# Inverse root by whole columns, sums and residual on GpSimd, held weights joining a step later, at the phase borders of a two-block layer kernel

## The chip, the cores and the metric

One core of one Trainium2 chip runs the whole kernel. The metric is the device time of one execution in microseconds; the time before is the median of three runs. A difference of about 0.3% (some 4.8 us) is what the measurement of this kernel can tell from none.

## The reference

Two transformer-like blocks are applied in turn to x (1 batch, 512 tokens, 1024 features), all in float32. What matters at the borders between the phases is only this:

```
# block 1 (g_t, g_c, sh_c, sc_c come from the conditioning vector c)
x = x + g_t * rms_norm(token_mixer(h, ...), tm_post_g)
h = rms_norm(x, cm_pre_g) * (1 + sc_c) + sh_c
x = x + g_c * rms_norm(conv_ffn(h, ...), cm_post_g)
# block 2
h = x
h = h + hybrid_mixer(rmsnorm(h, norm_mix_g), ...)
h = h + conv_ffn_2(rmsnorm(h, norm_ffn_g), ...)
return rmsnorm(h, norm_final_g)
```

Every normalisation needs 1/sqrt(mean of squares over the 1024 features + 1e-6) for each token. The token mixer has four branches (mLSTM, gated linear attention, a convolution branch and a short convolution); two of them, and the layer norm of the third, use the same root for their own norms.

## The kernel before, in words

Activations lie with features on the 128 partitions and tokens along the free dimension: 8 feature tiles of 128x512. A product with a weight is done in three TensorE products of rounded parts (high x high, high x low, low x high), so each weight tile of 128x1024 is loaded by a DMA that SyncE issues (`wraw`), copied by ScalarE into its high part (line 119) and subtracted by VectorE into its low part (line 120). `wload` does this through rings of three buffers; `hold` and `Group` do it into buffers kept for a while.

The instructions are put into each engine's queue by the Tile scheduler, at build time, from the order of the program and a model of what each instruction takes; each queue then runs in that fixed order on the chip. An instruction at the head of a queue that waits holds everything behind it.

There are three borders that the change concerns, each between the last product of one phase and the first of the next:

- border 1: end of the token mixer (`wo`), start of the first FFN (`up1`), near 484 to 537 us
- border 2: end of the first FFN (`dn1`), start of the second block's projections (`w2`), near 845 to 908 us
- border 3: end of the second mixer (`wo2`), start of the second FFN (`up2`), near 1214 to 1263 us

At each, the last few output tiles (4, 3 and 4) are done for tokens 0 to 255 and then for 256 to 511 (`HALVES`), so that the norm of the first half can run while TensorE works on the second.

`Post.add` (line 285 on) takes one output tile from PSUM. ScalarE writes y scaled by the gain (line 296) and two squares (lines 298, 301), VectorE adds the squares to two sums (lines 299, 302) and the product y*x to a third (lines 304, 305). `Post.rows` sums the three over the partitions on TensorE (`colsum`, line 240, a 128x1 product for each 128 tokens), takes two roots one after the other (`rsqrt`) and spreads them over the partitions by transposes on TensorE (`rowcast`, line 247). `advance` then adds the normed y to x (lines 917, 918, VectorE) and `normed` makes the next phase's input in two parts (lines 923, 927 and 928, or 923, 119 and 120).

`Group` (line 174 on) is the first product of the next phase: six weight tiles against each input tile k as soon as it is there. Three tiles come from `wload`; the other three are `slots`, split into memory that is free only once the phase before is over: at border 1 two tiles of the pool `sp4` and one tile of the FFN's activation buffer, at border 2 three tiles of `sth`/`stl`, at border 3 three tiles of the activation buffer. `step(k, half)` takes one slot from the list, issues its DMA and its two split instructions, appends it to the tiles in use, and then issues the products of all tiles in use, a newly joined tile catching up on the steps it has missed. In the second half the steps 4 to 6 are left to the last one, so that the six tiles finish one after another.

`rsqrt` (line 213 on) makes s = scale*src + eps, a first guess from the bits of s by two integer instructions, and then three Newton steps. For one or two columns it uses, for each column by itself, two VectorE instructions per step with a per-partition scalar (lines 227, 228); for more columns three instructions per step over all columns (lines 231 to 233). It is called with two columns at the borders (ten times), with four, eight or sixteen in the start and in the mixer of block 1 (five times), with one at the end (four times).

GpSimd has only memsets, a cast and causal masks to do. The temporaries of `Post.add` come from a ring: three buffers at border 1; at border 2 five, of which the three sums hold three.

## Time and profile before

| | us |
|---|---|
| median of 3 runs (1598.73, 1601.64, 1603.09) | 1601.64 |
| the profiled execution, its own time | 1603.05 |
| its span, first to last instruction | 1601.3 |
| TensorE busy in the span | 1568.9 (98%) |
| VectorE busy | 1083.4 (68%) |
| ScalarE busy | 677.5 (42%) |
| GpSimd busy | 15.9 (1%) |
| mean granted TensorE clock | 0.993 |

Line numbers are those of the kernel before. A row of a timeline gives the start in us from the span's start, the length, the engine, the line, the operation, the output tile and the input tiles by their names in the program, the shape, the count, and in square brackets how long the engine was idle before it and what ended that idle time. "PE" is TensorE, "DVE" VectorE, "ACT" ScalarE, "POOL" GpSimd. Two instructions that follow each other in a queue overlap at their edges, so the distance from start to start is what one of them takes from the engine, and it is a little shorter than the length shown.

### The profile page before, as it was taken

Reading aid. Unit: us, or ns where it says so; the run is one execution under the profiler, and the core shown is the slowest. Engines: PE = TensorE matmul, PEld = TensorE weight load, DVE = VectorE, ACT = ScalarE, POOL = GpSimd, SP = SyncE. Lnnn points to the kernel's source line nnn. Section 1 sums busy time; section 2 is a strip of 40 time slices with the busy share of each in tenths; the row PEclk is TensorE's granted clock in tenths of the full one; section 3 lists DMA queues with packets and bytes.
Section 4 is the critical chain, followed back from the end, with each engine's and each line's share of the span. In section 5 each row is a group of like instructions: output and inputs, shape, how many; then the busy total and the mean of one; then the engine's idle time right before and its main releaser. Section 6 shows DMA issues by size and latency. Waiting matters only on the chain.

```text
span 1601.3 us, 20852 instructions
## 1 busy us (share of the span) xinstructions
PE 1568.9 (98%) x8015; PEld 1316.4 (82%) x8015; DVE 1083.4 (68%) x2066; ACT 677.5 (42%) x1040; POOL 15.9 (1%) x43
## 2 busy tenths in 40 slices
PE   6999999999999999999999999999999999999997
PEld 4777888888889888888899978888889988888886
DVE  7786897657778865665358899977556565665234
ACT  4456432223463544443244463448343444444122
POOL 0000100000000000000000000000000000000000
PEclk9999999999999999999999999999999999999999
DMA  8411335554550223233345222220241232232331
GB/s 305 170 53 67 106 115 187 184 170 153 177 169 17 79 97 100 92 100 91 96 134 187 75 66 89 83 93 27 79 152 59 80 100 98 92 104 81 98 113 53
DMA packets 50963, 175.91 MB, mean 110 GB/s; under 512 B 5920, under 2 KB 6192, under 8 KB 50864
## 3 DMA queue, kind: packets, MB, share of 16 engines
q1 hardware_dynamic: 50864, 174.58, 33.3%
q8 instruction: 63, 1.03, 0.3%
q14 instruction: 36, 0.29, 0.1%
HBM read 172.46 MB, written 2.10 MB: 109 GB/s over the span
## 4 chain that ended last, share of the span: by engine, by line
PE 90%; DVE 5%; ACT 3%; DMA 1%; issue 1%; SPq 0%; ACTq 0%; DVEq 0%
PE acc L131 23%; PE acc L132 23%; PE acc L133 23%; PE acc L197 3%; PE acc L1340 3%; PE tp L1340 2%; PE pc L1250 1%; PE pa L197 1%; PE pc L197 1%; PE pb L197 1%; PE pb L1340 1%; PE pa L1340 1%; PE pc L1340 1%; DVE lo L120 1%; PE acc L157 1%
## 5 line engine op out<-in xcount | busy, mean ns | idle before, releaser
L120 DVE TENSOR_TENSOR lo<-raw,hi 128x1024 fp32r<-128x1024 f32 (+1 forms) x245 | 296.4, 1211 | 312.0 <-ACT hi L119 307.9
L131 PE MATMUL acc<-hh,hi 128*128 128x512 f32 x1208 | 474.3, 393 | 0.0
L133 PE MATMUL acc<-hh,lo 128*128 128x512 f32 x1208 | 473.1, 392 | 0.0
L132 PE MATMUL acc<-hl,hi 128*128 128x512 f32 x1208 | 473.1, 392 | 0.0
L119 ACT ACTIVATE hi<-raw 128x1024 fp32r<-128x1024 f32 (+1 forms) x245 | 257.1, 1050 | 471.1 <-PE acc L132 352.6
L131 PEld LDWEIGHTS acc<-hh,hi 128*128 128x128 f32 x1208 | 227.7, 189 | 48.9 <-issue 2.0
L132 PEld LDWEIGHTS acc<-hl,hi 128*128 128x128 f32 x1208 | 227.5, 188 | 48.6 <-issue 1.8
L133 PEld LDWEIGHTS acc<-hh,lo 128*128 128x128 f32 x1208 | 227.6, 188 | 47.5 <-issue 0.7
L131 PE MATMUL acc<-act_h,hi 128*128 128x256 f32 (+1 forms) x242 | 80.4, 332 | 0.0
L132 PE MATMUL acc<-act_l,hi 128*128 128x256 f32 (+1 forms) x242 | 80.2, 331 | 0.0
L133 PE MATMUL acc<-act_h,lo 128*128 128x256 f32 (+1 forms) x242 | 80.2, 331 | 0.0
L119 ACT ACTIVATE act_h<-ffe 128x512 fp32r<-128x512 f32 x44 | 27.7, 630 | 102.5 <-DVE ffe L968 102.5
L265 DVE SCALAR_TENSOR_TENSOR raw<-raw,cb 128x1024 f32<-128x1024 f32 x32 | 39.1, 1223 | 40.0 <-DMA raw<-in_ada_dram 40.0
L964 DVE SCALAR_TENSOR_TENSOR ffe<-acc,vec,ffe 128x510 f32<-128x510 f32 x82 | 61.2, 748 | 2.6
L967 ACT ACTIVATE ffe<-ffe 128x512 f32<-128x512 f32 x44 | 27.8, 631 | 79.5 <-DVE ffe L964 79.5
L962 DVE SCALAR_TENSOR_TENSOR ffe<-acc,vec,ffe 128x511 f32<-128x511 f32 x82 | 60.7, 742 | 0.0
L131 PEld LDWEIGHTS acc<-act_h,hi 128*128 128x128 f32 x242 | 46.0, 190 | 4.4
L133 PEld LDWEIGHTS acc<-act_h,lo 128*128 128x128 f32 x242 | 46.0, 190 | 4.3
L132 PEld LDWEIGHTS acc<-act_l,hi 128*128 128x128 f32 x242 | 46.0, 190 | 4.3
L120 DVE TENSOR_TENSOR act_l<-ffe,act_h 128x512 fp32r<-128x512 f32 x44 | 30.3, 690 | 26.5 <-ACT act_h L119 26.5
L808 DVE SCALAR_TENSOR_TENSOR cv<-u,vec,cv 128x512 f32<-128x512 f32 x60 | 43.8, 746 | 0.1
L197 PE MATMUL acc<-hl,hi 128*128 128x256 f32 x144 | 40.2, 285 | 0.0
(632 smaller groups left out, 2778.4 us busy)
## 6 DMA issues: line engine op xcount, KB each, us to landing
raw<-in_up_dram SPq DMA_DIRECT2D x88, 512.0 KB, 3.3
raw<-in_wg_dram SPq DMA_DIRECT2D x48, 512.0 KB, 3.3
raw<-in_dn_dram SPq DMA_DIRECT2D x44, 512.0 KB, 3.5
raw<-in_w_dram SPq DMA_DIRECT2D x43, 512.0 KB, 3.4
raw<-in_ada_dram SPq DMA_DIRECT2D x32, 512.0 KB, 3.4
sraw<-in_ada_dram SPq DMA_DIRECT2D x16, 512.0 KB, 5.3
raw<-in_wo_dram SPq DMA_DIRECT2D x16, 512.0 KB, 3.3
raw<-in_dn_dram SPq DMA_DIRECT2D x11, 384.0 KB, 3.2
```

The source lines that it names most:

```text
L119: A.activation(hi, src, AF.Copy)
L120: V.tensor_sub(lo, src, hi.bitcast(F32))
L131: T.matmul(out, wh_, ah, start=start, stop=False)
L132: T.matmul(out, wh_, al, start=False, stop=False)
L133: T.matmul(out, wl_, ah, start=False, stop=stop)
L197: T.matmul(a, w_, x_, start=(k == 0 and n == 0 and half == 0), stop=(k == KT - 1 and n == 2 and half == 1), skip_group_check=True)
L265: V.scalar_tensor_tensor(raw, raw, 1.0, cb, op0=ALU.mult, op1=ALU.mult, accum_out=mod[:, i:i + 1])
L808: V.scalar_tensor_tensor(cv[:, j], u0[:, j, k:k + 512], htap[:, 2 * k + j:2 * k + j + 1], cv[:, j], op0=ALU.mult, op1=ALU.add)
L962: V.scalar_tensor_tensor(t[:, 1:512], acc[:, 0:511], vcol(taps, 44 + i), t[:, 1:512], op0=ALU.mult, op1=ALU.add)
L964: V.scalar_tensor_tensor(t[:, 2:512], acc[:, 0:510], vcol(taps, i), t[:, 2:512], op0=ALU.mult, op1=ALU.add)
L967: A.activation(e[0], e[0], AF.Silu)
L1340: T.matmul(o, act[a][:, k, t], w[:, n0:n1], start=(k == 0 and i == 0), stop=(k == KF - 1 and i == 2), skip_group_check=True)
```

## The change

It has four parts.

1. `rsqrt` drops the path by single columns for two columns; the last two of the three Newton steps become one step of third order with constants built from RK. The number of instructions goes from 16 to 10 for two columns, from 10 to 9 for one (which keeps the scalar form), and from 12 to 10 for four and more.
2. In `Post.add`, for tiles of half the tokens only, the two adds of squares go from VectorE to GpSimd.
3. In `advance`, the add to x goes from VectorE to GpSimd (all 32 calls are on half the tokens).
4. In `Group.step`, a slot's DMA and split stay where they were in the program, but the tile is appended after the products of the step, so its first products are issued in the next step, where it catches up.

```diff
+RK = 1.5 ** (1.0 / 7.0)
...
         def step(self, k, half, act, nlast=4):
+            coming = None
             if self.todo:
-                w, src = self.todo.pop(0)
-                split(w[0], w[1], wraw(src))
-                self.w.append(w)
-            if half == 1 and KT - nlast <= k < KT - 1:
-                return
-            for m in range(len(self.w)):
-                for q in range(self.done[m][half], k + 1):
-                    self.mm(m, q, half, act)
-                self.done[m][half] = k + 1
+                coming, src = self.todo.pop(0)
+                split(coming[0], coming[1], wraw(src))
+            if not (half == 1 and KT - nlast <= k < KT - 1):
+                for m in range(len(self.w)):
+                    for q in range(self.done[m][half], k + 1):
+                        self.mm(m, q, half, act)
+                    self.done[m][half] = k + 1
+
+            if coming:
+                self.w.append(coming)
...
-        if n <= 2:
-
-            m = sm.tile([128, 2], F32, tag="rs_m", name="rs_m")[:, :n]
-            V.tensor_scalar(m, src, -0.5 * scale, -0.5 * EPS, op0=ALU.mult, op1=ALU.add)
-            for _ in range(3):
-                for c in range(n):
-                    yc, uc = y[:, c:c + 1], u[:, c:c + 1]
-                    V.scalar_tensor_tensor(uc, yc, m[:, c:c + 1], yc, op0=ALU.mult, op1=ALU.mult)
-                    V.scalar_tensor_tensor(yc, uc, 1.5, yc, op0=ALU.add, op1=ALU.mult)
-            return y
-        for _ in range(3):
+
+        if n == 1:
+            V.tensor_scalar(s, s, -0.5 * RK, None, op0=ALU.mult)
+            V.scalar_tensor_tensor(u, y, s, y, op0=ALU.mult, op1=ALU.mult)
+            V.scalar_tensor_tensor(y, u, 1.5 * RK, y, op0=ALU.add, op1=ALU.mult)
+            V.scalar_tensor_tensor(u, y, s, y, op0=ALU.mult, op1=ALU.mult)
+        else:
             V.tensor_tensor(u, y, y, op=ALU.mult)
-            V.scalar_tensor_tensor(u, u, -0.5, s, op0=ALU.mult, op1=ALU.mult)
-            V.scalar_tensor_tensor(y, u, 1.5, y, op0=ALU.add, op1=ALU.mult)
+            V.scalar_tensor_tensor(u, u, -0.5 * RK, s, op0=ALU.mult, op1=ALU.mult)
+            V.scalar_tensor_tensor(y, u, 1.5 * RK, y, op0=ALU.add, op1=ALU.mult)
+            V.tensor_tensor(u, y, y, op=ALU.mult)
+            V.scalar_tensor_tensor(u, u, -0.5 * RK, s, op0=ALU.mult, op1=ALU.mult)
+        V.scalar_tensor_tensor(u, u, RK ** 3 / 0.6, u, op0=ALU.add, op1=ALU.mult)
+        V.scalar_tensor_tensor(y, u, 1.25 * RK ** 6, y, op0=ALU.add, op1=ALU.mult)
         return y
...
-                V.tensor_tensor(s[0], s[0], t, op=ALU.add)
+                E = V if n == 512 else G
+                E.tensor_tensor(s[0], s[0], t, op=ALU.add)
...
-                V.tensor_tensor(s[1], s[1], t, op=ALU.add)
+                E.tensor_tensor(s[1], s[1], t, op=ALU.add)
...
         t = btmp()
         V.tensor_tensor(t, y[:, j, t0:t1], r1, op=ALU.mult)
-        V.tensor_tensor(x[:, j, t0:t1], x[:, j, t0:t1], t, op=ALU.add)
+        G.tensor_tensor(x[:, j, t0:t1], x[:, j, t0:t1], t, op=ALU.add)
```

## Rows read from the trace of the kernel before

**Rows 1.** The head of the profile's page: the span and the busy time of the engines.

```profile
span 1601.3 us, 20852 instructions
PE 1568.9 (98%) x8015; PEld 1316.4 (82%) x8015; DVE 1083.4 (68%) x2066; ACT 677.5 (42%) x1040; POOL 15.9 (1%) x43
```

**Rows 2.** The list of waits of TensorE over the whole span: the waiting line and what ended the wait, then us in total, times, longest us.

```profile
PE pc L197 <- ACT act_h L119: 1.2, 1, 1.2
...
PE pa L197 <- ACT sth L119: 0.7, 1, 0.7
...
PE pb L197 <- ACT sth L119: 0.4, 1, 0.4
```

**Rows 3.** Busy time of each engine in two stretches, one in border 1 and one in border 2: the stretch, its length, busy us and count for PE, PEld, DVE, ACT and POOL, the granted TensorE clock (1.00 is 2.4 GHz), the DMA share and GB/s.

```profile
497.00:508.00 11.00, 9.46 (x74) 8.68 (x72) 9.74 (x42) 3.92 (x8) 0.00 (x0) 1.00 0.13 40
...
868.00:882.00 14.00, 12.76 (x88) 11.95 (x88) 12.79 (x45) 5.98 (x10) 0.57 (x3) 0.88 0.66 203
```

**Rows 4.** Timeline of TensorE in border 1.

```profile
500.62 0.50 PE L240 MATMUL tp<-cst,th 128*128 128x1 f32 x4
502.32 0.38 PE L197 MATMUL pc<-hh,act_h 128*128 128x256 f32 x1 [1.20 <-ACT act_h L119]
```

**Rows 5.** Timeline of ScalarE in border 1: the split of the third slot and the instruction behind it.

```profile
501.21 1.06 ACT L119 ACTIVATE act_h<-raw 128x1024 fp32r<-128x1024 f32 x1 [2.64 <-PE tp L240]
502.17 0.49 ACT L927 ACTIVATE hh<-cb,mod 128x256 fp32r<-128x256 f32 x1
```

**Rows 6.** Timeline of VectorE in border 1.

```profile
495.27 0.42 DVE L304 TENSOR_TENSOR tmp<-y,x 128x256 f32<-128x256 f32 x1
...
496.28 0.42 DVE L305 TENSOR_TENSOR th<-th,tmp 128x256 f32<-128x256 f32 x1
496.61 0.47 DVE L923 SCALAR_TENSOR_TENSOR cb<-x,gcols,tp 128x256 f32<-128x256 f32 x1
...
499.53 0.47 DVE L923 SCALAR_TENSOR_TENSOR cb<-x,gcols,tp 128x256 f32<-128x256 f32 x1
```

**Rows 7.** Timeline of TensorE in border 2.

```profile
873.73 0.28 PE L197 MATMUL acc<-hh,lo 128*128 128x256 f32 x1
874.74 0.38 PE L197 MATMUL pa<-hh,sth 128*128 128x256 f32 x1 [0.74 <-ACT sth L119]
...
876.59 0.28 PE L197 MATMUL pa<-hl,sth 128*128 128x256 f32 x1
876.71 0.37 PE L197 MATMUL pa<-hh,stl 128*128 128x256 f32 x1
...
877.10 0.42 PE L197 MATMUL pa<-hl,sth 128*128 128x256 f32 x1
877.31 0.41 PE L197 MATMUL pa<-hh,stl 128*128 128x256 f32 x1
```

**Rows 8.** Timelines of VectorE and of ScalarE in border 2: the first two rows are VectorE's, the last two ScalarE's.

```profile
873.58 0.16 DVE L217 TENSOR_SCALAR rs_s<-tp 128x2 f32<-128x2 f32 x1 [1.19 <-PE tp L240]
...
873.85 0.47 DVE L923 SCALAR_TENSOR_TENSOR cb<-x,vec,tp 128x256 f32<-128x256 f32 x1
...
873.63 2.96 ACT L119 ACTIVATE sth<-raw 128x1024 fp32r<-128x1024 f32 x3 [3.30 <-PE tp L240]
876.49 0.40 ACT L119 ACTIVATE hh<-cb 128x256 fp32r<-128x256 f32 x1
```

**Rows 9.** Timelines of VectorE in three roots: of four columns in the convolution branch (371 us), of two columns in border 3 (1216 to 1218 us, first and last instruction, with one other instruction of 0.41 us between them), of one column at the end of the kernel (1595.7 us on), and ScalarE's first use of that one.

```profile
371.31 0.16 DVE L231 TENSOR_TENSOR rs_u<-rs_y 128x4 f32<-128x4 f32 x1
...
371.90 0.16 DVE L231 TENSOR_TENSOR rs_u<-rs_y 128x4 f32<-128x4 f32 x1
...
1215.91 0.16 DVE L217 TENSOR_SCALAR rs_s<-tp 128x2 f32<-128x2 f32 x1 [0.76 <-PE tp L240]
...
1217.75 0.41 DVE L1283 TENSOR_TENSOR x<-x,acc 128x256 f32<-128x256 f32 x1
1218.08 0.15 DVE L228 SCALAR_TENSOR_TENSOR rs_y<-rs_u,rs_y 128x1 f32<-128x1 f32 x1
...
1595.72 0.16 DVE L228 SCALAR_TENSOR_TENSOR rs_y<-rs_u,rs_y 128x1 f32<-128x1 f32 x1
1595.91 0.22 DVE L227 SCALAR_TENSOR_TENSOR rs_u<-rs_y,rs_m 128x1 f32<-128x1 f32 x1
...
1596.81 0.72 ACT L1369 ACTIVATE xt<-xt,rs_y 128x512 f32<-128x512 f32 x1 [2.14 <-DVE rs_y L228]
```

**Rows 10.** Timeline around the last root of the gated linear attention: VectorE's use of the root and the TensorE instruction that waited for it.

```profile
130.42 0.68 DVE L637 TENSOR_TENSOR go<-tp,rs_y 128x512 f32<-128x512 f32 x1
...
131.25 0.19 PE L674 MATMUL tp<-cst,rows 4*128 4x4 f32 x1 [0.81 <-DVE go L637]
```

**Rows 11.** Single lines of the program: the add to x, and one of the adds of squares (border 2's phase); engine, operation, tiles, count, then shortest, median and longest ns, first and last start, and shapes.

```profile
L918 DVE TENSOR_TENSOR x<-x,cb x32: 415/424/426, 494.9 to 898.1; 128x256 f32<-128x256 f32 x32
...
L302 DVE TENSOR_TENSOR ffe<-ffe x10: 414/417/684, 775.6 to 870.6; 128x256 f32<-128x256 f32 x6, 128x512 f32<-128x512 f32 x4
```

**Rows 12.** Timeline of GpSimd and VectorE in two places: the same masking instruction of GpSimd, once beside an instruction of VectorE that reads one of its two operands from PSUM (L732), once beside a weight split of VectorE.

```profile
161.24 0.29 POOL L721 TENSOR_SCALAR_AFFINE_SELECT x2a<-x2a 128x128 f32<-128x128 f32 x1 [0.74 <-ACT x2a L718]
...
960.84 1.22 DVE L120 TENSOR_TENSOR lo<-raw,hi 128x1024 fp32r<-128x1024 f32 x1
960.99 1.22 POOL L1116 TENSOR_SCALAR_AFFINE_SELECT mb<-mb 128x128 f32<-128x128 f32 x1 [7.14 <-DVE mb L1114]
```

## The prediction

> **What bounds the kernel now.** I read the head of the page first: TensorE is busy 1568.9 of 1601.3 us [rows 1]. So the change can only give back what TensorE waits for, and everything else is hidden. The list of TensorE's waits comes next: at the borders it names three waits for the held weights, 1.2 us at border 1 and 0.7 and 0.4 us at border 2 [rows 2]. Border 3 has no such row: there TensorE is fed. The windows of the two borders say the same from the other side: TensorE is idle 1.54 of 11 us at border 1 and 1.24 of 14 us at border 2, and in the second the granted clock is 0.88 [rows 3]. As the clock has two levels, 1.2 and 2.4 GHz, 0.88 means 3.4 of the 14 us at the lower.
>
> Then the timelines, to see who is late. At border 1 TensorE has done its column sums at about 501.1 us and starts again at 502.32 with the third slot's weights [rows 4]. ScalarE had begun that split at 501.21, because the memory came free only with the column sums, and the next tile's high part stood behind it in ScalarE's queue until 502.17 [rows 5], although its input left VectorE at 500.0 [rows 6]. So not only the weights are late: the next input tile waits behind them. At border 2 it is the same with three splits: ScalarE makes them in one piece of 2.96 us from 873.63 on, and the high part of the next input tile follows at 876.49 [rows 8]; TensorE stops at 873.85 (873.73 + 0.12) and gets its weights at 874.74 [rows 7]. VectorE is late too: it made the input of that tile at 873.85, after 1.19 us in which its queue stood at the root's first instruction, waiting for the column sums [rows 8].
>
> **Part 1, the root.** For two columns, 16 instructions become 10. That isn't six times their length. The old root ran from 1215.91 to 1218.23, less the 0.33 us of one foreign instruction in it: 1.99 us [rows 9], since the two columns' chains overlap. The new one is a chain of ten dependent instructions over whole columns. Three of these take 0.59 us (371.31 to 371.90), so 0.197 each and 1.97 us for ten [rows 9]. The root's own latency at the borders stays as it is: 0.0, with 0.2 us to either side. What it frees is VectorE's queue where other work is mixed in, and I count that under part 2. One column: one step less on the last chain. From the second half of one step to the first of the next is 0.19 us (1595.72 to 1595.91), and ScalarE's first use ends a wait of 2.14 us for the root, with nothing on TensorE [rows 9]: -0.2 us, fully on the path that sets the end. Eight columns: two instructions less, 0.39 us, ahead of the instruction at 130.42 that TensorE waits 0.81 us for [rows 10]: -0.4, between 0 (another queue entry is next) and -0.8. The other roots of four and sixteen columns stand beside TensorE's work or beside loads: 0.
>
> **Part 2, the sums on GpSimd.** 14 half tiles have two adds each: 28 leave VectorE (the row of one of the two lines shows 6 half tiles at border 2; border 1 has 8). For a half tile VectorE now needs 1.43 us from the start of its first add to the end of its last (495.27 to 496.70) [rows 6], and at border 1 such a block stood right ahead of the next phase's input at 496.61. With two of four instructions gone VectorE ends 0.68 us sooner. GpSimd's adds of two tensors have no row. The nearest are its mask over half the columns, 0.29 us by itself and 1.22 us beside a weight split of VectorE, both starting within 0.15 us [rows 12]. I take 0.6, twice the lower for twice the columns; ends 0.29 and 1.22. At 0.6 the second add ends 1.2 us after the first square is there, about where VectorE's last ended; at 1.22 it ends 1.2 us later than now. The column sums are next in TensorE's queue after that, and behind them stand the next phase's products, so a late sum is paid by TensorE. There are four such places (two halves, two borders): at 1.22 that is +5.0 us, at 0.29 -1; I take +0.2 each, +0.8 in all, because the scheduler places the sums by its model and nothing says that it fits GpSimd.
>
> The Trainium skill, GPSIMD Engine Reference, section 3.1, has 4497 ns for an add of 2048 float32 columns on GpSimd against 2293 ns on VectorE, and tells to keep such work on VectorE. An estimate from it, an eighth of that plus a fixed part, is 0.6 to 0.7 us for these adds, near the value that I take; by it the sum would come out less than half a microsecond higher. No run here shows it yet.
>
> **Part 3, the add to x.** 32 instructions of 0.42 us [rows 11] leave VectorE and one of GpSimd takes their place in the chain of each input tile. The chain gets longer by 0.2 (at 0.6) or 0.8 us (at 1.22), but VectorE's work per tile falls from four instructions to three, 1.58 to about 1.2 us. TensorE needs 18 products of 0.12 us, 2.2 us, per tile with six weights and 1.1 with three (spacing 876.59 to 876.71 [rows 7]). By the time of the column sums of the second half, VectorE has 2 us (two blocks of adds, two x adds) less to do at border 1 and as much at border 2, so one or two further input tiles, with their high parts, pass ScalarE before the splits. Each gives TensorE 9 to 15 products, 1.1 to 1.8 us. That covers the 1.20 us at border 1 (-1.2) and the 0.74 and 0.45 us at border 2 (-1.2). The cover is these tiles alone: if they don't pass, both waits stay.
>
> At border 2 the clock is the larger item. TensorE was idle 0.74 and 0.45 us, and then the spacing of its products went from 0.12 to 0.21 us (877.10 to 877.31) [rows 7]. In 3.4 us these are 16 products with 0.09 us too much: 1.5 us. With the idle gone, I take this back whole: -1.5, with 0 at the other end.
>
> **Part 4, the slots a step later.** DMA, ScalarE copy and VectorE subtraction of a slot keep their place in the program; no queue but TensorE's is passed. The products move behind those of the step, which by itself moves the wait rather than removes it: at border 1 the input tile behind the split came free at 502.66, later than the weights [rows 5]. So the step is worth what part 3 puts in front of it: 0 by itself, -0.3 to +0.3.
>
> **The sum,** against the profiled execution (1603.05, span 1601.3): -0.4 (eight columns) -0.2 (end) -1.2 (border 1) -1.2 -1.5 (border 2) +0.8 (sums) = -3.7. The profiled execution lies 1.4 above the median, so 1601.64 - 3.7 = **1597.9 us**, -0.23%. A measurement of this kernel tells a change of about 0.3%, 4.8 us, from none.
>
> **The rivals.**
>
> *The waits stay (it doesn't do what it says).* ScalarE's order is fixed when the program is built. If the splits again stand ahead of the next high part, TensorE waits as now, for the input in place of the weights. For it: rows 5 and 8, where just this happened to an input that was ready (border 1) or nearly (border 2). Against it: 2 us less on VectorE ahead of it. It leaves the root's 0.6 us and half a wait: **1601.0**. Chance 0.24.
>
> *Everything closes.* GpSimd's add is at 0.29: the four sums come sooner (-1 in place of +0.8), the linear attention's root gives its 0.8, and small waits of 0.2 go: -3.7 - 1.8 - 0.4 - 0.8 = -6.7: **1594.9**. For it: GpSimd is empty at the borders (0.57 us in 14) [rows 3]. Chance 0.18.
>
> *GpSimd is the new bound, and it is slower.* The mechanism is one: GpSimd and VectorE hold each other up where VectorE reads two operands from SBUF, as the mask beside the split shows, 1.22 in place of 0.29 us [rows 12]. Then an input tile costs 1.22 + 0.40 us one after the other (the low part reads two operands too), 1.62 against the 1.1 that three weight tiles give TensorE: 0.5 us for each of the first four tiles at two borders, 4.3 us, and +5.0 at the sums, -0.6 of the roots, no wait regained: **1610.3**. It decides from about 0.7 us for the add (1.1 - 0.40) on, and wins by more than 4.8 us from about 0.9. Against it: most of VectorE's work around the add to x (lines 917 and 923) reads one operand from PSUM, and the mask beside such work took 0.29. Chance 0.08.
>
> The Trainium skill, SBUF — State Buffer, section "SBUF: two separate sides", has the rule for this: the port pair that both engines share is a lock held for a whole instruction, against VectorE instructions with two SBUF inputs. By that rule this rival is right in kind wherever splits and low parts are mixed with GpSimd's adds; the trace agrees in the one place it shows (1.22 beside 0.29).
>
> **How the numbers follow.** The forecast has 0.50 and its own range of 1596.0 to 1600.0. Below 1596.8 (faster by 0.3%) lie the second rival's 0.18 and 0.15 of the forecast's: 0.33. Above 1606.4 lies the third, 0.08. The rest, 0.59, can't be told from no change. The range from 1593.5 to 1602.5 takes in the forecast and the first two rivals with their spread and leaves out the third and the tails, together less than 2 in 10.
>
> **What would show it.** Right: the rows of waits for act_h and sth are gone, ScalarE's splits at 501 and 873 have more high parts ahead of them, the granted clock stays 1.00 through border 2, GpSimd's adds take near 0.6 us, and the last root is 0.2 us shorter. Wrong: a wait of the column sums for a GpSimd line, a wait of TensorE for a high part that stands behind a split, GpSimd adds of 1 us and more, or a second fall of the clock at border 1. Each of these says which term failed.

## The result, and the profile after

The changed kernel takes 1618.93 us in the median, against 1602.37 us for the kernel before on the same chip: a ratio of 1.0101, 95% interval 1.0088 to 1.0115. It is slower by 16 us, and 21 us above the forecast. The median is of 1616.09, 1618.50, 1619.36 and a slow run of 2608.15 us at a mean granted clock of 0.557, which all ratios and intervals leave out, like two more further down (1730.62 us of e3_sums, and 4013.68 us of e10_ring, its profiled one, so that it has no windows in the table). The profiled execution's own time is 1616.09 us. In this section, lines are those of the changed kernel; against the listing of the kernel before they lie 1 to 4 further down (split L121, the products of `Group` L198, adds of squares L303 and L306, y*x L308 and L309, `advance` L921 and L922, next input L927, high part L931 or L120, low part L932 or L121, column sums L243, transposes L250). In the other kernels below they differ by a few lines again.

The busy times, which answer to [rows 1] (the span is 1614.4 us):

```profile
PE 1575.2 (98%) x8015; PEld 1322.4 (82%) x8015; DVE 1079.4 (67%) x1932; ACT 677.2 (42%) x1040; POOL 65.5 (4%) x103
```

134 instructions and some 25 us of adds left VectorE, and its busy time fell by only 4.0 us (from 1083.4): what stayed got longer. GpSimd took on 50 us. The list of waits of TensorE, which answers to [rows 2]:

```profile
PE acc L198 <- DVE lo L121: 3.7, 2, 2.4
...
PE tp L250 <- DVE rs_y L236: 2.2, 1, 2.2
...
PE acc L198 <- ACT tmp L301: 1.1, 1, 1.1
PE tp L243 <- POOL th L303: 0.8, 2, 0.5
...
PE tp L243 <- POOL ffe L303: 0.6, 1, 0.6
```

The three waits for held weights (2.3 us) are gone, as they were meant to. In their place stand 8.4 us at the borders: for low parts of weights (VectorE), for a root (VectorE), for a square of ScalarE and for GpSimd's sums. Busy time by engine and granted clock around the two borders, in the columns of [rows 3], but in wider stretches, so that they hold nearly the whole border of every kernel (here the last product of the `Group` at border 1 ends at 542.85 us):

```profile
480.00:540.00 60.00, 55.29 (x426) 53.57 (x425) 47.18 (x117) 19.90 (x42) 23.45 (x30) 0.94 0.07 22
845.00:925.00 80.00, 74.95 (x563) 71.94 (x562) 59.67 (x134) 30.33 (x52) 21.39 (x31) 0.94 0.40 126
```

TensorE is idle 4.71 us at border 1 and 5.05 at border 2 (kernel before, same stretches: 1.67 and 2.12), and the granted clock is 0.94 in both (1.00 and 0.98), that is at the lower of its two levels for about 7 of the 60 and 10 of the 80 us. From the first to the last product of the `Group` it takes 42.68 us at border 1 and 46.08 at border 2, against 38.88 and 39.94. Border 3, where nothing of this is on the path, takes 35.81 against 35.98.

Who got slower is in the groups of instructions (line, engine, operation, tiles, form, count; busy us and mean ns; idle us before them and what ended it):

```profile
L927 DVE SCALAR_TENSOR_TENSOR cb<-x,vec,tp 128x256 f32<-128x256 f32 x32 | 14.5, 474 | 5.7 <-POOL x L922 5.2 <-PE tp L250 0.5
L921 DVE TENSOR_TENSOR cb<-y,tp 128x256 f32<-128x256 f32 x32 | 13.1, 410 | 1.6 <-PE tp L250 1.6
L932 DVE SCALAR_TENSOR_TENSOR hl<-cb,mod,hh 128x256 fp32r<-128x256 f32 x16 | 12.4, 775 | 3.0 <-ACT hh L931 2.8
...
L308 DVE TENSOR_TENSOR ffe<-y,x 128x256 f32<-128x256 f32 x6 | 5.7, 942 | 4.8 <-POOL ffe L303 4.8
```

```profile
L922 POOL TENSOR_TENSOR x<-x,cb 128x256 f32<-128x256 f32 x32 | 26.1, 815 | 52.1 <-DVE cb L921 44.4 <-DVE rs_y L222 4.0 <-DVE rs_u L233 2.5
L306 POOL TENSOR_TENSOR th<-th,tmp 128x256 f32<-128x256 f32 x8 | 7.8, 978 | 0.0
```

The pattern is sharp. L921 and L927 read one operand from PSUM and take what they took before (0.41 and 0.47 us). L932 and L308 read both from SBUF and take 0.78 and 0.94 us in the mean, in place of 0.48 and 0.42. The timelines show it one by one; first border 1, GpSimd, VectorE and TensorE (the wait is in brackets):

```profile
492.98 0.72 POOL L303 TENSOR_TENSOR th<-th,tmp 128x256 f32<-128x256 f32 x1 [1.38 <-ACT tmp L301]
493.66 0.72 POOL L306 TENSOR_TENSOR th<-th,tmp 128x256 f32<-128x256 f32 x1
...
493.03 0.68 DVE L234 SCALAR_TENSOR_TENSOR rs_u<-rs_u,rs_s 128x2 f32<-128x2 f32 x1
493.75 0.65 DVE L235 SCALAR_TENSOR_TENSOR rs_u<-rs_u 128x2 f32<-128x2 f32 x1
494.43 0.16 DVE L236 SCALAR_TENSOR_TENSOR rs_y<-rs_u,rs_y 128x2 f32<-128x2 f32 x1
...
494.65 0.43 PE L250 MATMUL tp<-cst,rs_y 128*128 128x128 f32 x2 [2.18 <-DVE rs_y L236]
```

Two instructions of the root on 128x2 take 0.68 and 0.65 us in place of 0.16, each ending as one of GpSimd's two adds ends, and TensorE stands 2.18 us for that root. At border 2 it goes the other way round, GpSimd being held by VectorE:

```profile
878.65 0.48 DVE L927 SCALAR_TENSOR_TENSOR cb<-x,vec,tp 128x256 f32<-128x256 f32 x1 [0.84 <-POOL x L922]
879.04 1.22 DVE L121 TENSOR_TENSOR lo<-raw,hi 128x1024 fp32r<-128x1024 f32 x1
...
880.85 1.22 DVE L121 TENSOR_TENSOR lo<-raw,hi 128x1024 fp32r<-128x1024 f32 x1
...
877.88 0.73 POOL L922 TENSOR_TENSOR x<-x,cb 128x256 f32<-128x256 f32 x1 [2.40 <-DVE cb L921]
881.00 1.65 POOL L922 TENSOR_TENSOR x<-x,cb 128x256 f32<-128x256 f32 x1 [2.39 <-DVE cb L921]
...
880.32 0.58 PE L198 MATMUL acc<-hh,lo 128*128 128x256 f32 x1 [2.36 <-DVE lo L121]
```

GpSimd's add at 881.00 starts inside the split of 880.85 and ends at 882.65, 0.58 us after the split does: it stood behind it. VectorE's queue stands 0.84 us at L927 for the add to x, so the split of 879.04 behind it is late, and TensorE waits 2.36 us for that weight's low part. Its clock is at the lower level from 879.25 on, for 10.2 us.

The order that the prediction asked for did come. ScalarE has four high parts ahead of the third slot's split at border 1, where the kernel before had one, and seven or eight ahead of the three splits of border 2, where it had four. Border 1, before and after:

```profile
497.12 0.51 ACT L927 ACTIVATE hh<-cb,mod 128x256 fp32r<-128x256 f32 x1 [1.35 <-DVE cb L923]
```

```profile
497.17 0.51 ACT L931 ACTIVATE hh<-cb,mod 128x256 fp32r<-128x256 f32 x1 [3.97 <-DVE cb L927]
...
498.99 0.51 ACT L931 ACTIVATE hh<-cb,mod 128x256 fp32r<-128x256 f32 x1 [0.37 <-DVE cb L927]
501.85 0.51 ACT L931 ACTIVATE hh<-cb,mod 128x256 fp32r<-128x256 f32 x1 [2.34 <-DVE cb L927]
...
503.66 0.51 ACT L931 ACTIVATE hh<-cb,mod 128x256 fp32r<-128x256 f32 x1 [0.36 <-DVE cb L927]
508.61 1.06 ACT L120 ACTIVATE act_h<-raw 128x1024 fp32r<-128x1024 f32 x1 [4.44 <-PE tp L243]
```

That covers the waits for the held weights. But the split starts at 508.61 us, in place of 501.21 [rows 5], and ScalarE waits up to 3.97 us for its inputs. With one instruction less in each, the input tiles follow each other on VectorE not faster but more slowly. At the end of border 1, before and after:

```profile
523.75 0.47 DVE L923 SCALAR_TENSOR_TENSOR cb<-x,gcols,tp 128x256 f32<-128x256 f32 x1
...
525.33 0.47 DVE L923 SCALAR_TENSOR_TENSOR cb<-x,gcols,tp 128x256 f32<-128x256 f32 x1
```

```profile
528.10 0.47 DVE L927 SCALAR_TENSOR_TENSOR cb<-x,gcols,tp 128x256 f32<-128x256 f32 x1
...
529.92 0.47 DVE L927 SCALAR_TENSOR_TENSOR cb<-x,gcols,tp 128x256 f32<-128x256 f32 x1
```

From start to start a tile takes 1.82 us here, in place of 1.58, and at the end of border 2 it takes 1.83 in place of 1.51.

### The profile page after: what moved, and what is told of

Its sections match the earlier page's. It is cut to its first block, busy times and chain, and to the rows that moved or that the text cites. A ratio compares the mean times of both kernels' runs of the same rounds, so it can differ in the third digit from the quotient of the medians.

```text
span 1614.4 us, 20797 instructions
## 1 busy us (share of the span) xinstructions
PE 1575.2 (98%) x8015; PEld 1322.4 (82%) x8015; DVE 1079.4 (67%) x1932; ACT 677.2 (42%) x1040; POOL 65.5 (4%) x103
## 4 chain that ended last, share of the span: by engine, by line
PE 88%; DVE 7%; ACT 2%; issue 2%; POOL 1%; DMA 1%; SPq 0%; ACTq 0%; DVEq 0%; POOLq 0%
PE acc L132 22%; PE acc L133 22%; PE acc L134 22%; PE acc L1344 3%; PE acc L198 2%; PE tp L1344 2%; PE acc L158 1%; PE pc L1254 1%; PE pa L1344 1%; PE pb L1344 1%; PE pc L1344 1%; DVE lo L121 1%; PE pa L198 1%; PE pc L198 1%; PE pb L198 1%
## 5 line engine op out<-in xcount | busy, mean ns | idle before, releaser
L121 DVE TENSOR_TENSOR lo<-raw,hi 128x1024 fp32r<-128x1024 f32 (+1 forms) x245 | 296.4, 1211 | 318.0 <-ACT hi L120 307.5
L120 ACT ACTIVATE hi<-raw 128x1024 fp32r<-128x1024 f32 (+1 forms) x245 | 257.2, 1050 | 464.7 <-PE acc L133 354.6
L120 ACT ACTIVATE act_h<-ffe 128x512 fp32r<-128x512 f32 x44 | 27.7, 630 | 104.2 <-DVE ffe L972 104.2
L121 DVE TENSOR_TENSOR act_l<-ffe,act_h 128x512 fp32r<-128x512 f32 x44 | 30.4, 691 | 27.3 <-ACT act_h L120 27.3
L198 PE MATMUL acc<-hh,lo 128*128 128x256 f32 x144 | 42.9, 300 | 3.7 <-DVE lo L121 3.7
L198 PE MATMUL acc<-hh,hi 128*128 128x256 f32 x144 | 43.2, 300 | 1.4 <-ACT tmp L301 1.1
```

The source lines that it names most:

```text
L120: A.activation(hi, src, AF.Copy)
L121: V.tensor_sub(lo, src, hi.bitcast(F32))
L198: T.matmul(a, w_, x_, start=(k == 0 and n == 0 and half == 0), stop=(k == KT - 1 and n == 2 and half == 1), skip_group_check=True)
```

## The experiments

All are edits of the kernel before, timed against it. In every table line, "idle" is the time that TensorE was not busy and "clock" the granted clock, both from the windows of 480 to 540 us (border 1) and 845 to 925 us (border 2); "group" is the time from the first to the last product of `Group` there. These come from one profiled execution of each kernel: those of e7 (1609.61 us) and e9 (1611.93) are the shortest of their four, that of e13 (1602.76) is the longest of its ten. GpSimd's parts are the sums (S) and the add to x (X). Gains and losses in us are worked out from the ratios, times the kernel before's median of the same chip.

| kernel | median us | before us | ratio, 95% interval | border 1: idle, clock, group | border 2: idle, clock, group |
|---|---|---|---|---|---|
| before | 1601.64 | | | 1.67, 1.00, 38.88 | 2.12, 0.98, 39.94 |
| the change | 1618.93 | 1602.37 | 1.0101 [1.0088, 1.0115] | 4.71, 0.94, 42.68 | 5.05, 0.94, 46.08 |
| e1_root: root alone | 1598.45 | 1602.74 | 0.9975 [0.9963, 0.9988] | 0.52, 1.00, 38.08 | 2.33, 1.00, 38.52 |
| e2_slots: slots alone | 1602.25 | 1602.74 | 0.9999 [0.9989, 1.0008] | 1.55, 0.97, 39.56 | 2.13, 0.98, 39.94 |
| e3_sums: S alone | 1604.20 | 1602.74 | 1.0014 [1.0004, 1.0023] | 2.48, 0.97, 37.35 | 3.36, 1.00, 38.46 |
| e4_xadd: X alone | 1607.24 | 1602.74 | 1.0033 [1.0020, 1.0046] | 2.52, 0.97, 41.24 | 5.03, 1.00, 43.20 |
| e6_sums_xadd: S and X | 1617.95 | 1600.69 | 1.0107 [1.0092, 1.0122] | 4.86, 0.97, 41.16 | 6.38, 0.91, 46.54 |
| e7_no_slots: root, S, X | 1615.23 | 1600.69 | 1.0095 [1.0078, 1.0111] | 3.01, 0.91, 42.83 | 4.39, 0.91, 45.95 |
| e8_root_slots: root, slots | 1597.88 | 1600.69 | 0.9977 [0.9963, 0.9990] | 0.48, 1.00, 38.09 | 2.30, 1.00, 38.51 |
| e9_beside | 1616.96 | 1600.86 | 1.0093 [1.0068, 1.0118] | 4.79, 0.94, 43.39 | 5.45, 0.96, 45.52 |
| e10_ring | 1617.69 | 1600.86 | 1.0100 [1.0083, 1.0117] | | |
| e11_second_half | 1609.39 | 1600.86 | 1.0047 [1.0032, 1.0062] | 3.35, 0.97, 38.93 | 4.21, 0.96, 42.41 |
| e12_root_many | 1603.38 | 1600.86 | 1.0009 [0.9998, 1.0021] | 1.67, 1.00, 38.89 | 2.10, 0.98, 39.93 |
| e13_port_free | 1599.06 | 1601.96 | 0.9979 [0.9969, 0.9989] | 0.49, 1.00, 38.08 | 2.04, 1.00, 38.63 |

**The parts one by one.** e1_root to e4_xadd each take one part of the diff above, unchanged.

> The kernel before with the new root alone. Theory 'held up' (the loss is made by GpSimd's adds, which hold up VectorE instructions that read two operands from SBUF, and by VectorE's queue waiting for GpSimd): -1 to +1.5 us against before, no weight split of VectorE waited for at border 2, granted clock at border 2 as before or better. Rival 'order' (any edit makes the scheduler write another order, and that order is what costs; the shorter chain of the root moves splits and small instructions): +4 us or more already here, with the waits of TensorE for VectorE's root or low parts at the borders.

> The kernel before with the slots joining a step later, alone. Theory 'held up': -1.5 to +1.0 us against before; TensorE's waits for act_h and sth move to the next input tile's high part or shrink by some tenths. Rival 'order': +3 us or more at border 2, because the products that would have run during the wait stand behind.

> The kernel before with the two adds of squares of half tiles on GpSimd, alone. Theory 'held up': +3 to +8 us against before, GpSimd's adds at 0.7 to 1.0 us, VectorE's product y*x of border 2 waiting 0.3 to 1.3 us for GpSimd's add (the ring of temporaries), VectorE's other two-operand instructions stretched by up to 0.5 us, and a wait of TensorE at the column sums. Rival 'order': within 2 us of before.

> The kernel before with the add to x on GpSimd, alone. Theory 'held up': +3 to +9 us against before, VectorE's line 923 waiting 0.6 to 0.9 us for GpSimd's add wherever the next tile's work isn't ready, weight splits in VectorE's queue behind it late, TensorE waiting for those splits at border 2 and the clock falling there. Rival 'order': within 2 us of before.

The root gains 4.0 us (1.9 to 5.9), more than either theory of its expectation had. Its surest part is in the borders: 0.80 us of group at border 1, 1.42 at border 2, 0.17 at border 3, and 0.2 at the end (TensorE's last product to the end of the span: 7.98 in place of 8.18 us), 2.6 in all, and the rest is inside the interval; e8 and e13, which have the same root, repeat these within 0.2 us. In two of e1's ten executions (1594.59 and 1594.84 us) and in four of e8's ten the granted clock of the whole kernel was 0.999, where the kernel before had 0.991 to 0.997; no trace shows one of them, so what they add to the median is open. The waits of TensorE in e1_root, and its window at border 2:

```profile
PE pa L198 <- ACT sth L120: 0.7, 1, 0.7
...
PE pb L198 <- ACT sth L120: 0.4, 1, 0.4
...
PE pc L198 <- ACT act_h L120: 0.3, 1, 0.3
```

```profile
845.00:925.00 80.00, 77.67 (x558) 71.65 (x557) 73.44 (x177) 37.93 (x64) 1.63 (x7) 1.00 0.38 121
```

At border 2 both waits for held weights are still there and the idle time is no less than before, yet the clock stays at 1.00 (in e8 and e13 too): the fall that I had tied to those waits [rows 3, 7] goes without them going. At border 1 the wait for act_h falls from 1.2 to 0.3 us: two high parts stand ahead of its split in place of one.

Slots alone change nothing that can be told, and all three waits for the weights stay (1.2, 0.7 and 0.4 us). The sums alone shorten both groups, by 1.5 us each, and lengthen what lies ahead: TensorE waits 2.8 us for roots and 1.9 for GpSimd's sums. With them the waits for act_h and sth are gone, three high parts stand ahead of the split at border 1, and five or six ahead of those at border 2. The net is a loss of 2.2 us (0.6 to 3.7), which doesn't decide between the ranges of the two theories. The add to x alone costs 5.3, all of it in the groups (2.4 and 3.3 us); the wait of 1.2 us for act_h stays, with one high part ahead of the split as before, and the clock of border 2 doesn't fall, although its expectation had that.

**Combinations.**

> Both GpSimd parts, without the new root and without the later slots. The parts alone gave -4.0 (root), 0 (slots), +2.2 (sums), +5.3 us (add to x), 3.5 in sum, while the whole change gave +16. Theory 'GpSimd feeds on itself' (sums and adds to x stand in one GpSimd queue, each late one holds VectorE's queue, and the weight splits behind): +12 to +18 us against before here already. Rival 'the root and GpSimd' (the new root's ten dependent two-operand instructions over two columns are each held for a whole GpSimd add): +6 to +9 us here, the rest only with the root.

> The whole change without the later slots (root, sums and add to x). Theory 'GpSimd feeds on itself': +11 to +17 us against before, within 3 us of the whole change. Third possibility, that the slots joining later cost only where the input tiles come late: 5 us or more below the whole change.

> The change without anything on GpSimd (root and later slots). All theories that put the loss on GpSimd: -5.5 to -2.5 us against before, like the root alone (-4.0). If the slots cost something beside the shorter root: 0 us or above.

The two GpSimd parts alone give the whole loss and more: 17.1 us, where the sum of both by themselves is 7.5. The table shows where most of the other 9.6 is: at border 2 TensorE's idle time is 1.35 us more than with X alone, but the clock is 0.91 over 80 us, where each part alone kept 1.00; 0.09 of 80 is about 7 us of TensorE's work. At border 1 the idle time rises by 3.2 us, against 0.8 and 0.85 for the parts. Root and slots with nothing on GpSimd (-3.7 us) stand where the root alone stands, and without the slots the loss stays (+15.2): slots are worth nothing that can be told in either setting.

**The price by itself.** p1_port computes nothing of the reference: runs of equal instructions on each engine alone, then of both together, on tiles of 128x256 in SBUF, executed once. The code of one of the four pairs is shown; in the others VectorE adds two columns (128x2), multiplies with one operand in PSUM, or scales one tile by a constant.

```diff
+for _ in range(8):
+    G.tensor_tensor(go, ga, gb, op=ALU.add)
+for _ in range(12):
+    V.tensor_tensor(vo, va, vb, op=ALU.add)
```

> A kernel by itself that computes nothing of the reference: rows of instructions of GpSimd (adds of 128x256) and of VectorE, first each alone, then both at once, on tiles that have nothing to do with each other. Theory 'port' (GpSimd's add of two tensors and a VectorE instruction with two operands in SBUF exclude each other): the add of 128x256 on VectorE goes from 0.33 to about 0.7 us or more from start to start beside GpSimd's adds, the one of 128x2 from 0.07 or 0.2 to about 0.7, too, although it moves two columns; an instruction with one operand in SBUF and one in PSUM keeps its time. Rival 'dependence only': all keep their times, and the stretching in the whole kernel comes from waits.

Its timeline, GpSimd and VectorE; each row is a run of equal instructions (start, length of the whole run, count at the end). L45 to L57 are alone, L60 is GpSimd beside L62, and L67, L72 and L77 stand beside eight adds of GpSimd each:

```profile
5.40 6.32 POOL L45 TENSOR_TENSOR go<-ga,gb 128x256 f32<-128x256 f32 x8
12.19 5.49 DVE L48 TENSOR_TENSOR vo<-va,vb 128x256 f32<-128x256 f32 x12
18.22 2.31 DVE L51 TENSOR_TENSOR vo<-va,vb 128x2 f32<-128x2 f32 x12
20.96 6.16 DVE L54 SCALAR_TENSOR_TENSOR vo<-va,vc,acc 128x256 f32<-128x256 f32 x12
27.55 3.89 DVE L57 TENSOR_SCALAR vo<-va 128x256 f32<-128x256 f32 x12
31.97 8.70 DVE L62 TENSOR_TENSOR vo<-va,vb 128x256 f32<-128x256 f32 x12
32.52 6.95 POOL L60 TENSOR_TENSOR go<-ga,gb 128x256 f32<-128x256 f32 x8
41.21 4.43 DVE L67 TENSOR_TENSOR vo<-va,vb 128x2 f32<-128x2 f32 x12
48.18 6.16 DVE L72 SCALAR_TENSOR_TENSOR vo<-va,vc,acc 128x256 f32<-128x256 f32 x12
55.29 7.60 DVE L77 TENSOR_SCALAR vo<-va 128x256 f32<-128x256 f32 x12
```

Alone, an add takes 0.79 us of GpSimd (6.32/8; a single one lasts 0.72) and 0.46 of VectorE (5.49/12). Together both go in turns, at 0.87 us from start to start (6.95/8). A 128x2 add, 0.19 alone, takes 0.37 in the mean; the held ones last 0.57 to 0.64, a little less than the 0.7 expected. The instruction with one operand in PSUM doesn't change (6.16 and 6.16). The tensor_scalar, which has one operand in all, goes from 0.32 to 0.63 in the mean, which no expectation had. So the two engines hold each other up without any dependence between them.

**Contention or waiting?** In the changed kernel VectorE is held up at SBUF, and it also waits in its queue for GpSimd's results. e9_beside keeps only the first: the kernel of e1_root, VectorE doing all its adds itself, and near the same points (at y in place of its squares, and at each input tile) 60 GpSimd adds into a tile that nobody reads. The last two lines stand at border 2 as well.

```diff
                 V.tensor_tensor(s[2], s[2], t, op=ALU.add)
+                if n == 256:
+                    for _ in range(2):
+                        G.tensor_tensor(dum, z, z, op=ALU.add)
...
+                hd = h[0][:, j, t0:t1].bitcast(F32)
+                G.tensor_tensor(dum, hd, hd, op=ALU.add)
```

> The kernel with the new root alone (-4.0 us), all of whose own work stays where it was, and beside it as many GpSimd adds of 128x256 as the whole change has (two for each half tile, one for each input tile of borders 1 and 2), released at the same points but on a tile that nobody reads: their sums are thrown away. It takes VectorE's waits for GpSimd's results out and leaves the shared access to SBUF. Theory 'port alone': +8 us or more against before, most of the whole change's loss. Theory 'waits in VectorE's queue': within 0 to +4 us of the root alone, that is -4 to 0 against before; the stretched instructions are there, but the loss isn't.

It loses about as much as the change: 14.9 us (10.9 to 18.9), with nobody waiting for GpSimd. Its timeline at border 2, GpSimd and VectorE, and its list of TensorE's waits:

```profile
874.00 2.26 POOL L309 TENSOR_TENSOR dum<-y 128x256 f32<-128x256 f32 x2 [6.57 <-ACT y L297]
...
874.96 0.83 DVE L300 TENSOR_TENSOR ffe<-ffe 128x256 f32<-128x256 f32 x1
```

```profile
PE acc L198 <- DVE hl L933: 2.1, 5, 0.7
PE tp L248 <- DVE rs_y L234: 2.1, 3, 0.9
PE tp L241 <- DVE th L300: 1.7, 2, 1.3
```

VectorE's add takes 0.83 in place of 0.42, and TensorE waits for low parts, roots and sums of VectorE. So the shared access is enough for a loss of this size. It isn't a measure of its share in the change: VectorE has its 60 adds here as well, and in the change it waits some 11 us in all for results of GpSimd (L927 and L308). What these waits cost by themselves was not measured.

One doubt was left: instructions that hang on y and the input tiles could make the scheduler write another order. e13_port_free is e9 with each add replaced by a copy of one column, released at the same point, and a memset of about the same length (128x700, 0.68 us), which reads nothing from SBUF.

```diff
-                        G.tensor_tensor(dum, z, z, op=ALU.add)
+                        G.tensor_copy(dum[:, 0:1], z[:, 0:1])
+                        G.memset(dum, 0.0)
```

> The kernel of e9_beside (the new root, the rest of VectorE's work as before, and 60 GpSimd instructions at the same points that nobody waits for), except that each of the 60 adds of two tensors is replaced by a copy of one column (so that it is still released at the same point) and a memset of 700 columns of a tile that nobody reads: about as long on GpSimd (a memset of 512 columns took 0.52 us and one of 1024 columns 0.95 us in the kernel before, so an estimate of 0.68), but it reads no operand from SBUF. Theory 'GpSimd's adds of two tensors hold VectorE up through what both read from SBUF': VectorE's adds beside them take 0.42 us again, not 0.83, and the kernel stands where the root alone stands, 2 to 6 us faster than before. Rival 'the order': instructions that hang on the squares and on the input tiles make the scheduler write another order for all engines, and that order costs the time: VectorE's adds are at 0.42 us and yet the kernel is 8 us or more slower than before, as e9_beside was. Rival 'any GpSimd instruction holds VectorE up': VectorE's adds beside the memsets take clearly over 0.42 us, and the kernel is 8 us or more slower.

It stands where the root alone stands, 3.4 us faster than before. Timeline at border 2, and the window of border 1:

```profile
872.80 0.68 POOL L310 MEMSET dum<- 128x700 f32 x1
...
877.46 1.24 POOL L1044 COPY dum<-hh 128x1 f32<-128x1 f32 x1
...
872.96 0.42 DVE L306 TENSOR_TENSOR ffe<-ffe 128x256 f32<-128x256 f32 x1
...
877.45 1.21 DVE L121 TENSOR_TENSOR stl<-raw,sth 128x1024 fp32r<-128x1024 f32 x1
```

```profile
480.00:540.00 60.00, 59.51 (x480) 57.76 (x480) 50.45 (x157) 24.20 (x48) 30.34 (x64) 1.00 0.14 45
```

GpSimd is busier at border 1 than in the changed kernel (30.3 against 23.5 us), and VectorE's add inside a memset takes 0.42 us. The one-column copy, which does read SBUF, lasts 1.24 us beside a split of 1.21. And in the traces of e9 and e13 the instructions of VectorE, of ScalarE and of TensorE stand in the same order from first to last. So neither the number of GpSimd's instructions nor the order costs the time, but what they read.

The Trainium skill, SBUF — State Buffer, section "SBUF: two separate sides", states just this border: the shared pair is taken for a whole instruction, and a VectorE instruction with two SBUF inputs contends only with a GpSimd instruction that reads SBUF. The runs agree: 0.83 us beside adds, 0.42 beside memsets.

**Two side questions.** e10_ring gives the ring of temporaries of border 2 seven buffers in place of five, on top of e6 (in the changed kernel VectorE's L308 waits 4.8 us in all for GpSimd's reads of that ring).

```diff
-            return f1.tile([128, 512], F32, tag="ffe", name="ffe", bufs=5)
+            return f1.tile([128, 512], F32, tag="ffe", name="ffe", bufs=7)
```

> Sums and add to x on GpSimd as in the run that gave +17 us, with seven instead of five buffers in the first FFN's ring, so that four instead of two are left for the temporaries of the sums and VectorE's product y*x no longer has to wait for GpSimd's add. If this wait (0.3 to 1.3 us four times at border 2, with weight splits behind) carries the interaction of sums and add to x: +6 to +11 us against before. If it is one of many: +13 us or more.

16.0 us slower than before, as e6 within the intervals: two buffers more don't bring the loss down. No comparable trace shows whether the wait itself is gone. e11_second_half leaves the add to x of the first half on VectorE, again on top of e6:

```diff
-        G.tensor_tensor(x[:, j, t0:t1], x[:, j, t0:t1], t, op=ALU.add)
+        (G if t0 else V).tensor_tensor(x[:, j, t0:t1], x[:, j, t0:t1], t, op=ALU.add)
```

> Sums on GpSimd as in the run that gave +2.2 us, and the add to x on GpSimd only for the second half of the tokens, when no weight split of the phase before is left in VectorE's queue; in the first half it stays on VectorE. Theory 'what costs is VectorE waiting for GpSimd with weight splits behind it': +1 to +5 us against before, although half of the adds are there. Rival 'each add costs the same': half way between +2.2 and +17, +8 to +11.

With half of the adds to x moved the loss is 7.5 us (5.1 to 9.9), about half of e6's; it lies between the two ranges and decides for neither theory. e12_root_many keeps the old root for one and two columns and uses the new one only where it has four or more:

```diff
+        if n <= 2:
+            m = sm.tile([128, 2], F32, tag="rs_m", name="rs_m")[:, :n]
...
+            return y
```

> The new root for four and more columns only; for one and two columns the old one. The root alone gave -4.0 us. If the gain comes from the linear attention's root (the wait of 0.8 us and the fall of the clock behind it), as the prediction had it: -3 to -1.5 us. If it comes from the two columns at the borders: within 1 us of before.

No gain (+1.4 us, interval from -0.3 to +3.4), with the groups of the kernel before to 0.01 us. So the gain of the new root is that of two and one columns. The many columns do act where the prediction looked: from its 501st to its 751st product, the stretch with the roots of eight columns, TensorE takes 32.8 to 32.9 us in the seven traces with the new root there, and 34.3 to 35.9 in the six with the old one. But from the first product to the 501st the new root's traces need 109.0 to 116.4 us, the old one's 109.8 to 111.9. The start of the kernel can take the gain back; why it varies is open.

## Why the prediction was wrong

The forecast was 1597.9 us and the time is 1618.93: wrong in sign. By its steps:

**Part 1, the root (-0.6 forecast, -4.0 measured).** Right in sign, wrong in place. The -0.2 at the end came. The -0.4 of the eight columns isn't seen in the time: in e12 TensorE's wait of 0.8 us for them is gone, and the time isn't. The two columns, put at 0.0, carry the gain. Their chain was costed at 1.97 us against 1.99. In the trace of e1 a root is shorter than before by more than that, with the same foreign instructions inside: 2.14 us in place of 2.33 at border 3, 2.36 in place of 2.67 for the first one of border 1. And VectorE's queue is freer: in the root for the second half of border 1, at 500 us, nine instructions of other work stand in place of five, and a second high part passes ahead of the split. Both together give 2.4 us of the groups. At border 2 this is the fall of the clock that doesn't come; at border 3 the group is shorter by 0.17, about what the root is. How the 0.80 of border 1 divide between the shorter chain and the freer queue isn't separated.

**Part 2, the sums (+0.8 forecast).** The price of an add, taken at 0.6 with ends at 0.29 and 1.22, is 0.72 to 0.74 by itself and 0.73 to 0.98 in the mean of its lines. The step that failed is that VectorE's relief was counted as whole (0.68 us per half tile). Measured alone the sums give 3.0 us back in the groups and lose more ahead of them, mostly at a root that I had not thought to be exposed: instructions of one or two columns, held for a whole add each. That the forecast's +0.8 lies within the interval of the +2.2 measured is luck: neither of its two parts was in the sum at its size.

The estimate from the Trainium skill's GPSIMD Engine Reference, section 3.1, 0.6 to 0.7 us for such an add, was near (0.72 to 0.74 in the trace), and its advice to keep such work on VectorE holds in this case. The prediction's own slope from +0.8 at 0.6 to +5.0 at 1.22 makes the sum 0.7 us higher for an add of 0.7, not less than half a microsecond.

**Part 3, the add to x (-3.9 forecast, +5.3 measured alone, +14.9 on top of the sums).** The sentence that failed: "VectorE's work per tile falls from four instructions to three, 1.58 to about 1.2 us". It rises, from 1.58 to 1.82 us: the low part of the next tile takes 0.78 in the mean in place of 0.48 at border 1, and at border 2 L927 stands in VectorE's queue for 5.2 us in all, waiting for GpSimd's add. The high parts did pass ahead of ScalarE's splits, more of them than forecast, and the waits for the held weights did go. But it was the sums moved in part 2 that made them pass: with the add to x alone there is one ahead of border 1's split, as before, with the sums alone there are three. And what was taken as free cover wasn't: the 2.3 us of waits were replaced by 8.4.

**The clock (-1.5 forecast).** At border 2 it fell for longer, about 10 us, and at border 1 too, about 7 us. The prediction's own sign for this, "a second fall of the clock at border 1", stood among what would make the prediction wrong, as did column sums that wait for GpSimd and adds of 1 us. And the cause given to the fall in the kernel before, the waits for the weights, is refuted by e1_root, where the waits of border 2 stand and the clock doesn't fall. What in the shorter root keeps it up is open.

**Part 4, the slots (0).** Right: -0.2 us alone, +0.3 beside the root (e8 less e1) and +1.0 beside everything else (the change less e7), all inside what can be told.

**The rival with 0.08 won.** "GpSimd and VectorE hold each other up" is shown by e9 against e13, and by p1 without the kernel. Its point of decision, an add of 0.7 us, was met (0.72). Its price, +8.7, was half of the 16.2 measured: it counted the low parts and the sums, not the root's small instructions and not the clock. The reason held against it, that lines 917 and 923 read from PSUM, is true of those two lines (0.41 and 0.47 us) and was taken for the whole queue: between them stand low parts, splits, products and roots, which nearly all read two operands from SBUF. The row that showed it, 1.22 us beside a split [rows 12], was in hand and was used as the upper end of one add's price, where it was the sign of a rule for every pair.

The best kernel of these runs is the root alone: 0.9975 of the kernel before (0.9963 to 0.9988), with e8_root_slots beside it.

## What to carry to other kernels

Before work goes to an idle GpSimd, list what VectorE runs at that time by where its operands lie: against adds on GpSimd, whatever reads two operands from SBUF can last as long as the GpSimd instruction beside it, a two-column instruction too. Offloading then takes hardly anything off VectorE (1083.4 to 1079.4 us busy here, with 25 us of adds moved), and it makes the short latency chains of the queue long. And look beyond a chain's own length when it is shortened: here 0.2 to 0.3 us less in a root went with one more high part ahead of a split (0.80 us at border 1), and with a fall of the clock that didn't come (1.42 us at border 2).

## What the hardware showed that I had not expected

- A VectorE add of 128x2 takes 0.16 us, and 0.57 to 0.68 beside GpSimd's adds: size is no protection.
- A VectorE tensor_scalar on 128x256 float32 with one operand in SBUF goes from 0.32 to 0.63 us in the mean beside GpSimd's adds, though it reads only one tensor.
- It works both ways: a GpSimd copy of one column, 0.18 us alone in p1, lasts 1.24 beside a split of 1.21, and an add of 0.72 lasts 1.65.
- The losses of two parts don't add (7.5 us in sum, 17.1 together): in the profiled executions each alone kept the granted clock of border 2 at 1.00, and both together brought it to 0.91 over 80 us.
